# Splitting the last tile's quarter stores into 120 and 8 partitions in a batched 64 x 64 matmul

## The chip, the cores and the metric

The kernel runs on one core of one Trainium2 chip. The metric is the device time of one execution in microseconds (us), taken as the median of several executions. The core has five engines with a queue of instructions each: PE (matrix multiplication), DVE and ACT (elementwise work and copies), POOL and SP. POOL, SP and ACT also issue DMAs; the data of all of them is moved by the same 16 DMA engines.

## The reference

```python
a = np.random.randn(1024, 64, 64).astype(np.float32)
b = np.random.randn(1024, 64, 64).astype(np.float32)

def reference(a, b):
    return np.matmul(a, b).astype(np.float32)
```

1024 independent products of 64 x 64 matrices: 33.55 MB are read and 16.78 MB written.

## The kernel before, in words

The batch is cut into 16 tiles of 64 products (t = 0 to 15; n_t is 16). For a tile, b is loaded as 128 partitions (`load_b`, line 93, alternately on SP and ACT), and cast to bf16 (`cast`, line 140). Two tiles share one load of a (`load_a`, line 69), which is regrouped, transposed on PE against an identity (`transpose`, line 115) and spread by DVE into a block-diagonal form (`spread`, line 128). `multiply` (line 158) runs 64 matmuls of 128 x 64 per tile into PSUM, and `evacuate` (line 171; the copies are line 177) copies the results from PSUM into `o_sb`, a tile of 128 partitions with 8 groups `gh` of 256 fp32 each, so 1 KB per partition and group. In DRAM each of these 1 KB pieces is contiguous, and pieces of neighbouring groups are 128 KB apart.

The order of the work is written out by hand (`tc.manual_schedule()`); each engine's queue holds its instructions in that order. Stores are held back by one tile: `multiply` puts closures into `held[t]`, and `store` (line 154) calls them. Each calls `put(lo, n)` (line 165), which issues the DMA of groups lo to lo + n - 1 on line 166. `store_queue` (line 64) chooses the queue:

- tiles 0 to 13: one whole store of 1 MB each, on POOL;
- tile 14: two halves of 512 KB, both on SP;
- tile 15, the last: four quarters of 256 KB; the first and third (lo = 0 and 4) on ACT, the second and fourth (lo = 2 and 6) on SP.

The last tile's results are copied out of PSUM in the same four quarters, the first and third by ACT, the second and fourth by DVE (four copies of 64 x 256 for each), and a quarter's store waits for its copies.

The framework gives each DMA that is issued on SP or ACT one of eight completion semaphores, in turn. A DMA whose semaphore was used before first waits until that earlier DMA has landed. In the kernel before, tile 14's two stores have semaphores 3 and 4, and the four quarters 5, 6, 7 and 0; their previous users are loads that landed long before.

Of the kernel before, what the change touches and what calls it, by code (L numbers as in the profile page):

```python
# [13 lines left out]
def kernel(  # L14
# [27 lines left out]
    o_v = out.rearrange("(t gh x) (mo w) n -> t (x mo) gh (w n)", gh=8, x=8, w=4)  # L42
# [21 lines left out]
    def store_queue(t, lo):  # L64
        if t < n_t - 2:
            return nc.gpsimd
        return nc.scalar if t == n_t - 1 and lo % 4 == 0 else nc.sync
# [90 lines left out]
    def multiply(t):  # L158
        at_bd = bd_tiles[t % N_BD][:].rearrange("p j g wl h mo -> p j g (wl h mo)")
        at_bd = at_bd.bitcast(bf16).rearrange("p j g (c u) -> p j g c u", u=2)  # L160
        b_bf = bbf_tiles.pop(t)
        last = t == n_t - 1
        o_sb = o_pool.tile([128, 8, 2, 2, 64], fp32, name="o_sb")

        def put(lo, n):
            store_queue(t, lo).dma_start(  # L166
                out=o_v[t, :, lo : lo + n, :],
                in_=o_sb[:, lo : lo + n].rearrange("p gh j wl n -> p (gh j wl n)"),
            )

        def evacuate(o_ps, gh, n, copies):

            for par in range(2):
                for wl in range(2):
                    src = o_ps[64 * wl : 64 * wl + 64, :, par, :, :]
                    dst = o_sb[64 * par : 64 * par + 64, gh : gh + n, :, wl, :]
                    copies[2 * par + wl](dst, src)  # L177

        for half in range(2):
            if not last:  # L180
                o_ps = o_psum.tile([128, 4, 2, 2, 64], fp32, name="o_ps")
            for g8 in range(8):
                if last and g8 % 4 == 0:
                    o_ps = t_psum.tile([128, 2, 2, 2, 64], fp32, name="at_ps")
                g = 8 * half + g8
                gl = (g8 % 4 if last else g8) // 2
                for j in range(2):
                    for u in range(2):
                        nc.tensor.matmul(  # L189
                            o_ps[:, gl, g % 2, j, :],  # L190
                            at_bd[:, j, g, :, u],
                            b_bf[:, g, 64 * u : 64 * u + 64],
                            start=(u == 0),
                            stop=(u == 1),
                        )
                if last and g8 % 4 == 3:
                    copy = nc.scalar.copy if g8 == 3 else nc.vector.tensor_copy
                    evacuate(o_ps, g // 4 * 2, 2, [copy] * 4)
            if not last:
                copies = [nc.scalar.copy] * 4  # L200
                if half and t % 2:
                    copies[2:] = [nc.vector.tensor_copy] * 2
                evacuate(o_ps, 4 * half, 4, copies)
        if last:
            held[t] = [lambda q=q: put(2 * q, 2) for q in range(4)]
        else:
            whole = t < n_t - 2
            held[t] = [lambda q=q: put(q, 8 if whole else 4) for q in ([0] if whole else [0, 4])]
# [78 lines left out]
```

## Time and profile before

| what | value |
|---|---|
| median of 8 executions | 134.88 us (134.53 to 135.39) |
| the profiled execution, its own time | 134.85 us |
| its span, first to last instruction | 133.1 us |
| DVE busy | 94.7 us (71%) |
| ACT busy | 87.9 us (66%) |
| PE busy | 62.9 us (47%) |
| moved by DMA | 45.01 MB, mean 338 GB/s |
| quarter stores on SP: from issue to landing, median | 7.1 us |
| quarter stores on ACT: from issue to landing, median | 5.6 us |

The page of the profile shows one execution. Its second part cuts the span into 40 slices; a digit is the busy share of a slice in tenths. The third part lists the DMA queues (q0 is POOL's, q1 SP's and q10 ACT's; q8 and q14 fetch instructions) with packets, MB and the time that their packets took as a share of 16 engines' span. The fourth follows the chain of work that ended last back from the end. The fifth and sixth list groups of instructions and DMA issues by line. Other views cut the span into stretches that are chosen, or list what one line does in a window. In a fence, "x4" is a count of instructions.

### The profile page before, as it was taken

What the parts mean: (1) busy time and instruction counts of PE and PEld (TensorE: products, weight loads), DVE (VectorE), ACT (ScalarE), POOL (GpSimd) and SP (SyncE); (2) the same over time, 40 slices, a digit from 0 to 9 for tenths busy, and PEclk for the clock granted to TensorE, in tenths of its full rate; (3) what the DMA queues carried; (4) which work ended last, traced back from release to release, by engine and by line L of the source; (5) the groups of instructions that cost most, each with busy time, mean ns of one, the idle gap of its engine ahead of it and who ended that gap; (6) DMA issues with size and microseconds to landing.
All of it is one profiled execution on the core that took longest, in us unless ns stands there. A gap on an engine that the chain in (4) does not pass through costs nothing.

```text
span 133.1 us, 2837 instructions
## 1 busy us (share of the span) xinstructions
PE 62.9 (47%) x1152; PEld 59.8 (45%) x1152; DVE 94.7 (71%) x120; ACT 87.9 (66%) x161; POOL 33.1 (25%) x43
## 2 busy tenths in 40 slices
PE   0006306950089385099418960946098355861000
PEld 0006206940088375098418950935097354850000
DVE  5930499009998719994999799949999995988000
ACT  3125424999036999959495979585969969089800
POOL 8991000420090071252133021302120402210000
PEclk9999965896557999757985698699959955599555
DMA  3999999999999999999999999999999999999991
GB/s 70 373 335 310 306 313 277 284 306 328 324 304 404 320 322 328 399 384 398 316 280 368 408 390 358 305 310 386 393 398 388 394 393 392 401 403 401 381 341 38
DMA packets 19021, 45.01 MB, mean 338 GB/s; under 512 B 1088, under 2 KB 3136, under 8 KB 19008
## 3 DMA queue, kind: packets, MB, share of 16 engines
q0 software_dynamic: 6832, 20.19, 50.2%
q1 hardware_dynamic: 7120, 14.68, 30.5%
q10 hardware_dynamic: 5056, 9.96, 19.8%
q8 instruction: 9, 0.15, 0.4%
q14 instruction: 4, 0.03, 0.1%
HBM read 33.55 MB, written 16.78 MB: 378 GB/s over the span
## 4 chain that ended last, share of the span: by engine, by line
DMA 54%; DVE 14%; ACT 13%; PE 7%; issue 5%; SPq 1%; ACTq 0%; DVEq 0%
DMA b_sb<-in_b_dram 54%; ACT o_sb L177 9%; DVE at_bd L133 6%; PE o_ps L189 4%; DVE o_sb L177 3%; PE at_ps L120 3%; DVE b_bf L144 3%; ACT at_sb L123 2%; ACT b_bf L144 1%; SPq L90 1%; DVE a_bf L108 1%; ACT b_bf L151 1%; DVE a_bf L111 0%; SPq L96 0%; ACTq L166 0%
## 5 line engine op out<-in xcount | busy, mean ns | idle before, releaser
L177 ACT COPY o_sb<-o_ps 64x512 f32<-64x512 f32 x106 | 61.5, 580 | 10.6 <-PE o_ps L189 9.3
L189 PEld LDWEIGHTS <-at_bd 128*128 128x128 bf16 x1024 | 41.8, 112 | 41.0 <-DVE b_bf L144 26.6
L189 PE MATMUL o_ps<-b_bf,at_bd 128*128 128x64 bf16 x960 | 42.0, 215 | 36.8 <-DVE b_bf L144 24.7
L133 DVE COPY at_bd<-at_sb 32x1024 f32<-32x1024 f32 x64 | 47.0, 734 | 14.0 <-ACT at_sb L123 11.9
L166 POOL DMA_DIRECT2D out_dram<-o_sb x14 | 15.7, 1122 | 56.6 <-ACT at_sb L123 23.1
L120 PE MATMUL at_ps<-identity,a_bf 128*128 128x128 f32 x128 | 20.3, 326 | 19.3 <-ACT a_bf L105 11.1
L120 PEld LDWEIGHTS at_ps<-identity,a_bf 128*128 128x128 f32 x128 | 18.5, 174 | 19.3 <-issue 19.3
L144 DVE CAST b_bf<-b_sb 128x2048 bf16<-128x2048 f32 x14 | 17.9, 1276 | 9.9 <-DMA b_sb<-in_b_dram 9.7
L123 ACT COPY at_sb<-at_ps 128x512 f32<-128x512 f32 x32 | 17.5, 589 | 10.2 <-PE at_ps L120 7.5
L73 POOL DMA_DIRECT2D a_sb<-in_a_dram x21 | 13.4, 652 | 26.6 <-DVE a_bf L108 19.0
L177 DVE COPY o_sb<-o_ps 64x512 f32<-64x512 f32 x14 | 9.6, 689 | 0.3
L108 DVE COPY a_bf<-a_sb 128x3072 bf16<-128x3072 bf16 x7 | 6.7, 951 | 0.0
L105 ACT CAST a_bf<-o_sb 128x1024 bf16<-128x1024 f32 x2 | 2.1, 1045 | 5.1 <-DMA o_sb<-in_a_dram 5.1
L111 DVE CAST a_bf<-a_raw 128x1024 bf16<-128x1024 f32 x7 | 4.8, 685 | 0.0
L144 ACT CAST b_bf<-b_sb 128x2048 bf16<-128x2048 f32 x1 | 1.9, 1897 | 4.1 <-DMA b_sb<-in_b_dram 4.1
L217 DVE MEMSET at_bd<- 128x4096 f32 x1 | 3.5, 3472 | 0.8 <-issue 0.8
L105 DVE CAST a_bf<-o_sb 128x1024 bf16<-128x1024 f32 x2 | 2.7, 1355 | 1.8 <-DMA o_sb<-in_a_dram 1.8
L177 DVE COPY o_sb<-at_ps 64x256 f32<-64x256 f32 x8 | 3.4, 421 | 0.5 <-PE at_ps L189 0.4
L151 ACT CAST b_bf<-b_sb 128x512 bf16<-128x512 f32 x2 | 1.1, 615 | 3.5 <-DMA b_sb<-in_b_dram 3.5
L177 ACT COPY o_sb<-at_ps 64x256 f32<-64x256 f32 x8 | 2.9, 366 | 0.1
L214 ACT ACT_TABLE_LOAD x1 | 1.3, 1283 | 2.3 <-issue 2.3
L189 PE MATMUL at_ps<-b_bf,at_bd 128*128 128x64 bf16 x64 | 2.0, 193 | 1.2 <-DVE at_bd L133 1.2
(12 smaller groups left out, 6.1 us busy)
## 6 DMA issues: line engine op xcount, KB each, us to landing
out_dram<-o_sb POOLq DMA_DIRECT2D x14, 1024.0 KB, 21.7
a_sb<-in_a_dram POOLq DMA_DIRECT2D x21, 256.0 KB, 16.2
a_raw<-in_a_dram SPq DMA_DIRECT2D x7, 512.0 KB, 18.7
o_sb<-in_a_dram SPq DMA_DIRECT2D x2, 512.0 KB, 5.9
o_sb<-in_a_dram ACTq DMA_DIRECT2D x2, 512.0 KB, 7.1
out_dram<-o_sb SPq DMA_DIRECT2D x2, 512.0 KB, 6.9
out_dram<-o_sb SPq DMA_DIRECT2D x2, 256.0 KB, 7.1
out_dram<-o_sb ACTq DMA_DIRECT2D x2, 256.0 KB, 5.6
```

Of the source, the lines that this page charges most:

```text
L73: nc.gpsimd.dma_start(out=a_sb[:, h, :, :].rearrange("p v k -> p (v k)"), in_=a_v[s, h])
L105: copy(a_bf[:, :, h, :], a_sb[h].rearrange("p (v k) -> p v k", v=16))
L108: nc.vector.tensor_copy(a_bf[:, :, 0:3, :], cast_sb[:].rearrange("p h v k -> p v h k"))
L111: nc.vector.tensor_copy(a_bf[:, :, 3, :], raw[:])
L120: nc.tensor.transpose(at_ps[:, vo, :], a_cols[:, 4 * vo + 2 * j + wl, :], identity[:])
L123: nc.scalar.copy(at_tiles[s][:, j, :, wl, :, :], at_ps[:].rearrange("p vo (g mp) -> p g mp vo", mp=4),)
L133: nc.vector.tensor_copy(bd[rows, :, :, :, h, :].rearrange("p j g wl mo -> p j (g wl) mo"), at_tiles[t // 2][rows, :, half, :, :, :].rearrange(
L144: (nc.vector.tensor_copy if t else nc.scalar.copy)(b_bf[:], b_sb[:])
L166: store_queue(t, lo).dma_start(out=o_v[t, :, lo : lo + n, :], in_=o_sb[:, lo : lo + n].rearrange("p gh j wl n -> p (gh j wl n)"),)
L177: copies[2 * par + wl](dst, src)
L189: nc.tensor.matmul(o_ps[:, gl, g % 2, j, :], at_bd[:, j, g, :, u], b_bf[:, g, 64 * u : 64 * u + 64], start=(u == 0), stop=(u == 1),)
L217: nc.vector.memset(bd_tiles[0][:], 0.0)
```

## The change

`put` takes its 128 partitions in one store as before, unless the tile is the last one. For the last tile it issues two stores one behind the other on the same queue: partitions 0 to 119, and partitions 120 to 127.

```diff
         def put(lo, n):
-            store_queue(t, lo).dma_start(
-                out=o_v[t, :, lo : lo + n, :],
-                in_=o_sb[:, lo : lo + n].rearrange("p gh j wl n -> p (gh j wl n)"),
-            )
+
+            cuts = [0, 120, 128] if last else [0, 128]
+            for p0, p1 in zip(cuts[:-1], cuts[1:]):
+                store_queue(t, lo).dma_start(
+                    out=o_v[t, p0:p1, lo : lo + n, :],
+                    in_=o_sb[p0:p1, lo : lo + n].rearrange(
+                        "p gh j wl n -> p (gh j wl n)"
+                    ),
+                )
```

The stores are line 169 of the changed kernel. Its last tile has eight stores instead of four: on ACT the first quarter's large and small piece, then the third's; on SP the second's and then the fourth's. With the two halves of tile 14 ahead of them, ten stores take the eight semaphores in turn: 3 and 4 (tile 14), then 5 and 7 (second quarter, large and small), 6 and 0 (first quarter), 1 and 3 (fourth), 2 and 4 (third). The listing of the built program shows these waits:

```
SP   120x2x256 second quarter, large  [waits DMAHW5, DVE]
SP   8x2x256   second quarter, small  [waits DMAHW7]
SP   120x2x256 fourth quarter, large  [waits DMAHW1, DVE]
SP   8x2x256   fourth quarter, small  [waits DMAHW3]
ACT  120x2x256 first quarter, large   [waits DMAHW6, Activation]
ACT  8x2x256   first quarter, small   [waits DMAHW0]
ACT  120x2x256 third quarter, large   [waits Activation]
ACT  8x2x256   third quarter, small   [waits DMAHW4]
```

## The prediction

> **What bounds the kernel now.** I read the page from the top down: the 40 slices, the queue table, the chain, the issues; then the stretches of the tail, the DMA view of the last microseconds, and the stores one by one.
>
> ```profile
> DMA  3999999999999999999999999999999999999991
> ...
> q8 instruction: 9, 0.15, 0.4%
> ...
> DMA 54%; DVE 14%; ACT 13%; PE 7%; issue 5%; SPq 1%; ACTq 0%; DVEq 0%
> ```
>
> The DMA engines are nine tenths busy or more from the second slice to the last but one: the kernel is a stream of 45.01 MB, and compute only decides what is in the stream. 54% of the chain is a DMA. The chain stops at 125.85 us with an ACT copy; behind it only stores are left. The q8 line matters below: nine instruction fetches take 0.4% of 16 x 133.1 us, so about 0.95 us each (8.5 / 9), and a packet is on one engine.
>
> The tail by stretches (us from the span's start; busy time of PE, PEld, DVE, ACT, POOL; clock, DMA share, GB/s):
>
> ```profile
> 124.00:126.00 2.00, 0.00 (x0) 0.00 (x0) 0.00 (x0) 1.79 (x5) 0.00 (x0) 0.50 1.06 384
> 126.00:128.00 2.00, 0.00 (x0) 0.00 (x0) 0.00 (x0) 0.00 (x0) 0.00 (x0) 0.50 1.08 379
> 128.00:129.00 1.00, 0.00 (x0) 0.00 (x0) 0.00 (x0) 0.00 (x0) 0.00 (x0) 0.50 1.01 350
> 129.00:130.00 1.00, 0.00 (x0) 0.00 (x0) 0.00 (x0) 0.00 (x0) 0.00 (x0) 0.50 0.65 229
> 130.00:131.00 1.00, 0.00 (x0) 0.00 (x0) 0.00 (x0) 0.00 (x0) 0.00 (x0) 0.50 0.20 69
> 131.00:132.00 1.00, 0.00 (x0) 0.00 (x0) 0.00 (x0) 0.00 (x0) 0.00 (x0) 0.50 0.02 8
> ```
>
> From 126 us on no engine computes. All 16 DMA engines are full until 128.6 or so, then they run dry one after the other over 2.7 us. The DMA view of 128.0 to 131.4, in slices of 85 ns, shows how it ends:
>
> ```profile
> GB/s 374 386 362 374 373 386 386 338 325 301 301 277 265 253 253 277 265 229 217 217 193 193 181 181 169 133 84 72 72 60 36 24 24 24 24 24 24 24 24 0
> ```
>
> The last eight slices, from 130.63 to 131.31, hold 24 GB/s, a sixteenth of the 380 before: one engine alone, about 0.7 us behind all others. 24 GB/s is 1,024 B in 43 ns. Why one engine is late the same view for 112 to 134 us suggests: one of the nine q8 packets falls in it (0.3% of 16 x 22 us, 1.06 us). The profile names no engine.
>
> When the stores land I take from the instructions of line 166, cut to a window that holds one each: first the second half of tile 14 (SP), then the last quarter (SP), then the third quarter (ACT).
>
> ```profile
> L166 SPq DMA_DIRECT2D out_dram<-o_sb x1: 378/378/378, 122.8 to 122.8; - x1
> ...
> DMA to landing us min/median/max: 6.6/6.6/6.6
> ```
> ```profile
> L166 SPq DMA_DIRECT2D out_dram<-o_sb x1: 1244/1244/1244, 124.7 to 124.7; - x1
> ...
> DMA to landing us min/median/max: 7.1/7.1/7.1
> ```
> ```profile
> L166 ACTq DMA_DIRECT2D out_dram<-o_sb x1: 379/379/379, 125.9 to 125.9; - x1
> ...
> DMA to landing us min/median/max: 5.7/5.7/5.7
> ```
>
> So tile 14's second half lands at about 129.45, the third quarter at 131.6, the last quarter at 131.75; the remaining 1.35 us to 133.1 are the closing waits and barrier. The execution's own time is 134.85, 1.75 more than its span and 0.03 under the median of 134.88.
>
> **What the Trainium skill says.** (1) DMA: Bandwidth & Descriptors, section on why a DMA increments its semaphore by 16: a DMA runs on the largest number of engines, at most 16, that divides the slowest dimension of both sides, on the lowest-numbered ones. 128 gives 16, 120 gives 15, 8 gives 8. The trace of before has only 128 and cannot confirm it. So engine 15 gets nothing of the last tile, 0 to 7 get one partition more, 8 to 14 the same as now. (2) Same page, Latency and other measured facts: engines 7 and 15 are usually slower in traces. Here one engine is late, but which is not told. (3) SBUF, Door 1: partitions share 16 DMA ports, four by four, of some 27 GB/s each. With 128 partitions each engine has its own port by the page; how 120 are dealt to 15 is not said, and no run here shows it.
>
> **The change, part by part.** *Removed*: four stores of 128 x 2 pieces of 1 KB, 16 on each engine per quarter, 64 in all. *Added*: four stores of 120 x 2 (16 pieces on each of engines 0 to 14) and four of 8 x 2 (two on each of 0 to 7). Compute is unchanged in kind and order; the listings of both programs differ only by the four extra stores. Bytes are the same, 1 MB.
>
> *Engine 15*: 64 x 43 ns = 2.7 us less. It is worth something only if it is the late one. *Engines 0 to 7*: 4 x 2 x 43 ns = 0.34 us more. *Engines 8 to 14*: nothing.
>
> *Issues.* One store costs its queue 0.38 to 1.26 us (SP's four: 0.39, 0.38, 1.26, 1.24; ACT's: 0.40, 0.38). On SP the small piece of the second quarter stands ahead of the last quarter, which goes out 0.4 to 1.3 us later, at 125.0 to 125.9. That is hidden: SP's ring holds data on every engine until 128.6, and with 2 us to its first byte (below) it arrives by 128. If that cover went, the quickest engines would idle for some tenths, and they are 2.7 us ahead of the end. On ACT the small piece of the first quarter goes out behind the large one at about 124.8; the copies of the third quarter (124.73 to 125.85) are already handed to the engine, so that the third quarter's store still goes at 125.9. If they were not, 0.4 us later, still within the 2.7.
>
> *The added waits.* Eight semaphores are used in turn, and a store waits until its semaphore's previous DMA has landed. With ten stores at the end instead of six, the last two go round: the listing of the changed program has the small piece of the last quarter (SP) wait for tile 14's first half (landed 120.45 + 7.2 = 127.65), that of the third quarter (ACT) for tile 14's second half, 129.45. Behind each only the closing waits are queued; but these are what the end waits for. Time to the first byte after an issue: the first load of the kernel, 1.4 us (issued at 0.74, first bytes in the slice of 2.1); ACT's first quarter, 1.9 (issued at 124.36; its queue has no packet to 126.27 and one by 126.32); SP's tile 14, 2.65 (issued at 120.45, first packet by 123.12). I take 1.9, the same queue in the same tail, and keep 1.4 and 2.65. From last byte to landing: 131.31 to 131.7, about 0.35. So ACT's small piece lands at 129.45 + 0.1 (two added packets ahead of tile 14's on eight engines) + 0.05 + 1.9 + 0.09 (two packets) + 0.35 = 131.95, between 131.45 and 132.7, against 131.75 now. SP's could land 1.8 earlier, so its packets just follow its ring's backlog.
>
> *Regrouping.* If eight neighbouring partitions go to one engine, engines can meet at a port. From below nothing (no gain can come of it, the ports being one to an engine now); from above, half of the 2.7 us at some 13 instead of 24 GB/s, +1.0 us. I take 0.1, since the last engine runs alone and neighbours fall out of step.
>
> *Sum.* The late engine is among the lower eight: 131.75 + 0.34 = 132.1. ACT's small piece, due at 131.95, queues behind that engine's own last packets and adds no more. With 0.1 for regrouping the end moves 0.44: 134.85 + 0.44 = 135.3.
>
> **The rivals.** *A, faster: the spared engine is the late one.* The others end at 130.63; with 0.34 on the lower eight and 0.35 to landing, 131.3. Tile 14's second half then lands up to 0.7 earlier on the spared engine (16 packets of ACT's no longer between), and ACT's small piece lands at about 131.3 to 131.5. 134.85 - 0.45 = 134.4 (134.1 to 134.65). It decides if the late engine is number 15. For it: (2). Against: the lateness looks like an instruction fetch, about which nothing ties it to 15.
> *B, nearly nothing*: the late engine is one of 8 to 14, or the split does not fall on 15 engines. Only ACT's wait counts, 131.95: 135.05.
> *C, much slower*: ACT's small piece needs SP's 2.65 us, landing at 132.7, or the ports cost the upper bound: +0.95, 135.8. For it: 2.65 is a store of this kernel. Against: by 129.5 the rings are nearly empty.
>
> **How the numbers follow.** Forecast 0.40 (own range 135.0 to 135.6), A 0.30, B 0.12, C 0.18. About 0.3%, 0.40 us, can be told from no change: faster means under 134.48, slower over 135.28. Forecast: 0.25 slower, 0.15 same. A: 0.20 faster, 0.10 same. B: same. C: slower. Together 0.20, 0.37, 0.43. The range runs from 134.3, inside A, to 135.9, the end of C; some 0.15 is left outside.
>
> **What would show it.** Right: the last 24 GB/s stretch is longer or later by 0.3, and the last small store on ACT is issued at about 129.5 and lands near 132. Wrong by A: the lone engine's stretch is gone, and the last landing is before 131.5. By B: the stretch unchanged. By C: DMA share down between 126 and 130, or two empty microseconds ahead of the last 16 KB.

## The result and the profile after

The changed kernel takes 135.9 us (median of 11 runs, 135.52 to 136.53) against 134.95 (32 runs) of the kernel before: a ratio of 1.0073, 95% interval 1.0056 to 1.0091. It is slower by 0.95 us. The forecast was slower by about 0.4; rival C gave this size, 0.95, but not by what came about; the part on the prediction takes this up. The profiled execution took 135.52 us, the quickest of all, with a span of 133.7; in the trace the difference is therefore 0.67 and not 0.95.

The page after, slices and chain:

```profile
DMA  3999999999999999999999999999999999999982
...
DMA 54%; DVE 15%; ACT 13%; PE 6%; issue 5%; SPq 1%; ACTq 0%; DVEq 0%
```

Up to the last copy nothing has moved: ACT's last copy ends at 125.86, before at 125.85. The tail in stretches (columns as in the forecast: us; PE, PEld, DVE, ACT, POOL; clock, DMA share, GB/s):

```profile
124.00:126.00 2.00, 0.00 (x0) 0.00 (x0) 0.00 (x0) 1.80 (x5) 0.00 (x0) 0.94 1.05 377
126.00:128.00 2.00, 0.00 (x0) 0.00 (x0) 0.00 (x0) 0.00 (x0) 0.00 (x0) 0.50 0.97 293
128.00:129.00 1.00, 0.00 (x0) 0.00 (x0) 0.00 (x0) 0.00 (x0) 0.00 (x0) 0.50 0.69 202
129.00:130.00 1.00, 0.00 (x0) 0.00 (x0) 0.00 (x0) 0.00 (x0) 0.00 (x0) 0.50 0.94 269
130.00:131.00 1.00, 0.00 (x0) 0.00 (x0) 0.00 (x0) 0.00 (x0) 0.00 (x0) 0.50 0.89 294
131.00:132.00 1.00, 0.00 (x0) 0.00 (x0) 0.00 (x0) 0.00 (x0) 0.00 (x0) 0.50 0.23 77
```

Two things are new. From 126 to 128 us the engines are still busy (0.97), but they move 293 GB/s where it was 379: the same pieces of 1 KB take longer (by the trace's packet records 54 ns in the mean, 46 before). And from 128 to 129 they are idle for three tenths, where they were full. The DMA view of 128.0 to 131.4 has no lone engine at its end any more; in that stretch the engines are still at work together:

```profile
GB/s 205 205 205 193 181 205 169 181 169 217 265 229 241 241 205 205 229 289 289 265 313 325 325 337 313 277 265 337 337 362 301 289 277 253 229 169 133 145 145 73
```

The stores of line 169, one to a window, show why there is a gap. SP's small piece of the second quarter and then the large piece of the last quarter:

```profile
L169 SPq DMA_DIRECT2D out_dram<-o_sb x1: 1681/1681/1681, 124.7 to 124.7; - x1
```
```profile
L169 SPq DMA_DIRECT2D out_dram<-o_sb x1: 1790/1790/1790, 126.5 to 126.5; - x1
...
DMA to landing us min/median/max: 5.4/5.4/5.4
```

ACT's small piece of the first quarter, the large piece of the third, and the small piece of the third:

```profile
L169 ACTq DMA_DIRECT2D out_dram<-o_sb x1: 1990/1990/1990, 125.0 to 125.0; - x1
```
```profile
L169 ACTq DMA_DIRECT2D out_dram<-o_sb x1: 1320/1320/1320, 127.1 to 127.1; - x1
...
DMA to landing us min/median/max: 5.2/5.2/5.2
```
```profile
L169 ACTq DMA_DIRECT2D out_dram<-o_sb x1: 283/283/283, 129.6 to 129.6; - x1
```

The first small piece on each queue, 16 KB, holds it for 1.7 and 2.0 us; the two last large pieces are issued at 126.5 and 127.1 instead of 124.7 and 125.9. The last small piece goes out at 129.6, right after tile 14's second half has landed (129.57 by the trace's completion records, which note each engine's arrival for each store). Its first arrival is at 131.44 and its last at 132.64, the last of all; before, the last arrival was at 131.72. The same records count 15 arrivals for a piece of 120 partitions and 8 for a piece of 8, beside those that are noted at the issue.

### The profile page after: what moved, and what is told of

It is laid out like the page before. It is cut to its first block, busy times and chain, and to the rows that moved or that the text cites. A ratio compares the mean times of both kernels' runs of the same rounds, so it can differ in the third digit from the quotient of the medians.

```text
span 133.7 us, 2841 instructions
## 1 busy us (share of the span) xinstructions
PE 66.7 (50%) x1152; PEld 63.7 (48%) x1152; DVE 94.6 (71%) x120; ACT 88.0 (66%) x161; POOL 33.2 (25%) x43
## 4 chain that ended last, share of the span: by engine, by line
DMA 54%; DVE 15%; ACT 13%; PE 6%; issue 5%; SPq 1%; ACTq 0%; DVEq 0%
DMA b_sb<-in_b_dram 54%; ACT o_sb L182 9%; DVE at_bd L133 7%; PE o_ps L194 4%; DVE b_bf L144 4%; DVE o_sb L182 3%; PE at_ps L120 2%; ACT at_sb L123 2%; ACT b_bf L144 1%; SPq L90 1%; DVE a_bf L108 1%; ACT b_bf L151 1%; ACTq L169 0%; DVE a_bf L111 0%; SPq L96 0%
## 5 line engine op out<-in xcount | busy, mean ns | idle before, releaser
L194 PEld LDWEIGHTS <-at_bd 128*128 128x128 bf16 x1024 | 43.5, 114 | 39.1 <-DVE b_bf L144 26.3
L120 PE MATMUL at_ps<-identity,a_bf 128*128 128x128 f32 x128 | 22.5, 351 | 18.9 <-ACT a_bf L105 11.1
L120 PEld LDWEIGHTS at_ps<-identity,a_bf 128*128 128x128 f32 x128 | 20.8, 190 | 19.0 <-issue 19.0
L123 ACT COPY at_sb<-at_ps 128x512 f32<-128x512 f32 x32 | 17.5, 590 | 10.5 <-PE at_ps L120 7.6
L194 PE MATMUL at_ps<-b_bf,at_bd 128*128 128x64 bf16 x64 | 3.6, 241 | 1.0 <-DVE at_bd L133 1.0
```

The lines of the kernel that those rows point to most:

```text
L120: nc.tensor.transpose(at_ps[:, vo, :], a_cols[:, 4 * vo + 2 * j + wl, :], identity[:])
L123: nc.scalar.copy(at_tiles[s][:, j, :, wl, :, :], at_ps[:].rearrange("p vo (g mp) -> p g mp vo", mp=4),)
L194: nc.tensor.matmul(o_ps[:, gl, g % 2, j, :], at_bd[:, j, g, :, u], b_bf[:, g, 64 * u : 64 * u + 64], start=(u == 0), stop=(u == 1),)
```

## The experiments

Three theories stood after the profile. **Theory 1, blocked queue**: the small stores hold the large ones back and the engines run short. **Theory 2, grouping**: 120 partitions on 15 engines move slower. **Theory 3, the wait**: the last small stores wait for tile 14 and end last. Each run below was timed beside the kernel before, whose median was 134.94 to 135.03; ratios are to it, with 95% intervals.

### The large pieces first

```diff
-            held[t] = [lambda q=q: put(2 * q, 2) for q in range(4)]
+            held[t] = [
+                lambda q=q, part=part: put(2 * q, 2, part)
+                for part in (slice(0, 1), slice(1, 2))
+                for q in range(4)
+            ]
```

(`put` issues only the piece that `part` names.)

> All eight stores of the changed kernel, but on each queue the two large pieces go ahead of the two small ones. Theory 1 (blocked queue: in the changed kernel a small store holds its queue for 1.7 to 2.0 us, so that the large store behind it goes out 1.2 to 1.8 us late and the engines run short of data at 128 to 129 us): the large stores go out as before the change, at 124.7 and 125.9, the share at 128 to 129 is near 1 again, and most of the 0.95 us comes back, 135.0 to 135.3. Theory 2 (grouping: 120 partitions on 15 engines move slower): stays at 135.9. Theory 3 (the wait for tile 14's landing puts the last small store at the end): the wait is still there, stays at 135.8 to 135.9.

Measured: 137.27 us, ratio 1.0178 (1.0160 to 1.0196). All three theories miss it: the order that should have mended the loss more than doubles it. Its stretches:

```profile
126.00:127.00 1.00, 0.00 (x0) 0.00 (x0) 0.00 (x0) 0.00 (x0) 0.00 (x0) 0.50 0.98 302
127.00:128.00 1.00, 0.00 (x0) 0.00 (x0) 0.00 (x0) 0.00 (x0) 0.00 (x0) 0.50 0.93 248
128.00:129.00 1.00, 0.00 (x0) 0.00 (x0) 0.00 (x0) 0.00 (x0) 0.00 (x0) 0.50 0.97 276
129.00:130.00 1.00, 0.00 (x0) 0.00 (x0) 0.00 (x0) 0.00 (x0) 0.00 (x0) 0.50 0.92 281
130.00:131.00 1.00, 0.00 (x0) 0.00 (x0) 0.00 (x0) 0.00 (x0) 0.00 (x0) 0.50 0.48 125
131.00:132.00 1.00, 0.00 (x0) 0.00 (x0) 0.00 (x0) 0.00 (x0) 0.00 (x0) 0.50 0.26 79
132.00:133.00 1.00, 0.00 (x0) 0.00 (x0) 0.00 (x0) 0.00 (x0) 0.00 (x0) 0.50 0.18 53
```

The gap at 128 to 129 is closed, as theory 1 said, and it does not help. The engines are busy at 250 to 300 GB/s, and then a few of them go on alone, the last until 133.9. Theory 1 as the cause of the loss falls.

### Half of the split, two ways

```diff
-            cuts = [0, 120, 128] if last else [0, 128]
+            cuts = [0, 120, 128] if last and lo >= 4 else [0, 128]
```

> Only the third and fourth quarter are split; the small pieces are the last of their queues, and with eight stores at the end none waits for a store of tile 14. Theory 1: nothing stands behind the small pieces, 134.95 to 135.2. Theory 2: half of the loss, about 135.4. Theory 3: the wait is gone, 134.95.

Measured: 136.06 us, ratio 1.0077 (1.0056 to 1.0098). Nothing is held and nothing waits, and yet the whole loss is there, twice what theory 2 gave for it. The other half:

```diff
+            cuts = [0, 120, 128] if last and lo < 4 else [0, 128]
```

> Only the first and second quarter are split; each small piece stands ahead of a whole quarter of 128 partitions, and none waits for a store of tile 14. Theory 1: the quarters behind go out 1.2 to 1.8 us late as in the changed kernel, 135.5 to 135.9. Theory 2: half of the loss, about 135.4. Theory 3: 134.95.

Measured: 135.48 us, ratio 1.0037 (1.0023 to 1.0051): half the loss, as theory 2 said; theory 1's range began at 135.5, so that this run alone does not tell the two apart.

### The large pieces alone

```diff
+            cuts = [0, 120] if last else [0, 128]
```

> The last tile's quarters store only partitions 0 to 119; the last 8 partitions of that tile are left out, so 64 KB are not stored. Theory 1: no small store, nothing blocked, 134.8 to 134.95. Theory 2: the loss stays, 135.6 to 135.9. Theory 3: no wait, 134.8 to 134.95. If the engine that ends last in the kernel before is the one that is spared by 120 partitions, the last landing comes 0.4 to 0.7 earlier: 134.3 to 134.5.

Measured: 136.49 us, ratio 1.0122 (1.0093 to 1.0151). Four stores as before, no small one, no added wait, 64 KB less to move, and 1.51 us slower (136.49 - 134.98). Of the three only theory 2 expected a loss, and this one is above its range.

```profile
126.00:128.00 2.00, 0.00 (x0) 0.00 (x0) 0.00 (x0) 0.00 (x0) 0.00 (x0) 0.50 0.96 284
128.00:129.00 1.00, 0.00 (x0) 0.00 (x0) 0.00 (x0) 0.00 (x0) 0.00 (x0) 0.50 0.95 262
129.00:130.00 1.00, 0.00 (x0) 0.00 (x0) 0.00 (x0) 0.00 (x0) 0.00 (x0) 0.50 0.80 216
130.00:131.00 1.00, 0.00 (x0) 0.00 (x0) 0.00 (x0) 0.00 (x0) 0.00 (x0) 0.50 0.39 123
131.00:132.00 1.00, 0.00 (x0) 0.00 (x0) 0.00 (x0) 0.00 (x0) 0.00 (x0) 0.50 0.25 87
132.00:133.00 1.00, 0.00 (x0) 0.00 (x0) 0.00 (x0) 0.00 (x0) 0.00 (x0) 0.50 0.16 56
```

Busy engines move less (284 GB/s at 0.96), and they end far apart: a share of 0.25 from 131 to 132 is four engines of sixteen. The completion records say the same: of the last quarter's 15 arrivals (and one at the issue) eleven are in by 130.78, the other four at 131.73, 132.43, 133.00 and 133.27; the third quarter's last is at 133.60. Before, 15 of the last quarter's 16 were in by 130.26, the last at 131.72. While the four go on alone, after 132 us, each of their 1 KB packets takes 46 ns, as before the change: they fell behind earlier.

### What in the grouping costs

Eight stores of all 128 partitions, by group instead of by partition:

```diff
-            held[t] = [lambda q=q: put(2 * q, 2) for q in range(4)]
+            held[t] = [lambda q=q: put(q, 1) for q in range(8)]
```

(with the queue of each quarter kept).

> The last tile's quarters are each split by group instead of by partition: eight stores of 128 partitions x 1 KB, two where the changed kernel has a large and a small one, on the same queues in the same order. Theory 2 in the form that the runs so far leave (ports: 120 partitions are dealt to 15 engines in neighbouring eights, so that engines meet at the same SBUF ports): all 16 engines keep their own ports, and only the time that the added stores hold their queues is left, 135.0 to 135.4. Theory 1 (the number of stores on a queue is what costs): as the changed kernel, 135.8 to 136.0.

Measured: 134.76 us, ratio 0.9990 (0.9980 to 1.0000). Twice the number of stores costs nothing, though the later ones are issued late here too and the last waits for tile 14's second half (issued at 129.27). Then a cut at 64:

```diff
+            cuts = [0, 64, 128] if last else [0, 128]
```

> As the changed kernel, but cut at partition 64: two pieces of 64 partitions, each on all 16 engines (four partitions for each). Ports theory: each piece reaches only half of the ports, two engines at one port all the time, slower than the changed kernel: 136.5 to 138, with a busy share near 1 at about 200 to 250 GB/s. Rival (what costs is that only 15 engines carry the large piece and only 8 the small one): both pieces use 16 engines evenly, 135.0 to 135.4.

Measured: 134.91 us, ratio 0.9993 (0.9980 to 1.0006). The ports theory missed the time. But its last store, when it is alone, does what it said (same columns):

```profile
131.10:131.30 0.20, 0.00 (x0) 0.00 (x0) 0.00 (x0) 0.00 (x0) 0.00 (x0) 0.50 1.03 220
```

All engines are busy, and 220 GB/s come of it. The last store of the split by group holds as many bytes, from all 128 partitions, and moves 357 GB/s at the same share:

```profile
130.20:130.40 0.20, 0.00 (x0) 0.00 (x0) 0.00 (x0) 0.00 (x0) 0.00 (x0) 0.50 1.04 357
```

The Trainium skill, SBUF - State Buffer, Door 1, gives 218 GB/s as what the 8 ports of partitions 0 to 63 can carry; the last piece here is partitions 64 to 127, again 8 ports by that page. So engines do meet at ports, by that count two at each. Here it costs no time, most likely because the engines share the slowing evenly: the records of the last store have all 16 arrivals between 131.76 and 132.00, where before one engine came 1.5 us after the others.

```diff
+            cuts = [0, 112, 128] if last else [0, 128]
```

> As the changed kernel, but cut at partition 112: 112 and 16 partitions, both divisible by 16, so that each piece is on all 16 engines (seven partitions and one). Ports theory: seven neighbouring partitions for an engine share ports as eight do, 135.7 to 136.5. Rival (15 engines instead of 16): 135.0 to 135.3.

Measured: 135.58 us, ratio 1.0043 (1.0028 to 1.0058), a little under the range of the ports theory and above the rival's.

```diff
+                queue = nc.gpsimd if p0 else store_queue(t, lo)
```

> As the changed kernel, but the four small pieces go out on POOL's queue, which is idle by then. SP and ACT have only the large pieces, nothing is held, and no store waits for a store of tile 14. Theory 1 and theory 3: 134.9 to 135.2. Ports theory: nothing keeps the large pieces of the two queues apart, so as the kernel with the large pieces alone, 136.3 to 136.8.

Measured: 136.99 us, ratio 1.0164 (1.0138 to 1.0190). That is above the range: without the holding it is worse still. (The small pieces are late themselves on POOL, 7.1 us from issue to landing, but the last of them is in at 133.40 and the third quarter's large piece at 133.89.)

### Places in DRAM, or engines, or neighbours

The next two write the last tile's 1 KB pieces to other places of its own 1 MB, partitions 4 KB apart instead of 1 KB: once 128 partitions, once 120.

```diff
+    o_moved = out.rearrange("(t y) m n -> t (y m n)", y=64)[n_t - 1].rearrange(
+        "(g p q r) -> p g q r", p=128, g=2, q=4
+    )
...
-                    out=o_v[t, p0:p1, lo : lo + n, :],
+                    out=o_moved[p0:p1, :, lo // 2, :] if last else o_v[t, p0:p1, lo : lo + n, :],
```

> The kernel before, but the last tile's 1 KB pieces go to other places of the tile's own 1 MB in DRAM (neighbouring partitions 4 KB apart instead of 1 KB, the two groups of a quarter 512 KB apart), so the last tile's results are permuted. It is the control of the next run. If the places in DRAM don't matter: 134.9 to 135.1. If pieces that are written at the same time hinder each other by their places in DRAM: another time, slower or faster, which can't be foretold.

> As the control with moved places in DRAM, but only partitions 0 to 119 of the last tile's quarters are stored, on 15 engines; the last 8 partitions are left out and the rest of the tile is permuted. SBUF side (engines meet at the ports that their neighbouring partitions share): the places in DRAM make no difference, the loss against the control is the 1.0 to 1.8 us of the run with the large pieces alone, 136.0 to 136.8. DRAM side (15 engines that start 8 KB apart): with 32 KB between them the loss is another, most likely under 0.5 us: 134.9 to 135.5.

Measured: the control 134.99 us, ratio 1.0002 (0.9989 to 1.0015); with 120 partitions 136.26, ratio 1.0075 (1.0048 to 1.0102). The loss against the control is 1.3 us by the medians and 1.0 by the ratios, at other places too. So these places in DRAM are not the cause, which speaks for the SBUF side.

```diff
+            cuts = [0, 60, 120] if last else [0, 128]
```

> The last tile's quarters are stored as partitions 0 to 59 and 60 to 119, each piece on 15 engines with four neighbouring partitions for each; the last 8 partitions are left out. The number of stores, the holding of the queues and the waits are as in the cut at 64. Neighbouring eights as the cause: with four to an engine it goes as the cut at 64, 134.7 to 135.2. Fifteen engines as such as the cause: as the run with the large pieces alone, 135.8 to 136.5.

Measured: 134.77 us, ratio 0.9986 (0.9975 to 0.9998). Fifteen engines cost nothing when each has four partitions of a piece. The DMA view of this kernel, 128.0 to 132.4 in slices of 110 ns, says two things more:

```profile
GB/s 289 326 372 326 345 298 317 270 214 270 326 307 261 214 168 214 186 196 177 102 102 19 28 28 168 242 279 205 140 130 37 28 19 19 0 0 0 0 0 0
```

At 130.3 to 130.6 one engine works alone (19, 28, 28), as in the kernel before. By the completion records 14 of 15 engines are done with a piece of the second quarter by 128.88 and the last at 130.38: in this execution the late engine is one of the fifteen, not the spared one, and sparing one engine all of the last tile gains 0.14%, at most 0.25%. And behind it comes a second wave, from 130.64 on: the last store, which had waited for tile 14's second half (landed at 129.77). Here the wait is in full view.

### How the loss of the changed kernel is made up

```diff
+            cuts = ([0, 120, 128] if lo < 4 else [0, 120]) if last else [0, 128]
```

> The changed kernel without the small pieces of the third and fourth quarter, whose 8 partitions are left out: eight stores at the end, none waits for a store of tile 14, and the small pieces of the first and second quarter still hold the queues. If the wait of the last small stores is part of the loss: 135.4 to 135.6. If it is hidden: 135.8 to 136.0. If it is worth nothing that the later large stores are held back: as the large pieces alone, 136.3 to 136.6.

Measured: 135.54 us, ratio 1.0046 (1.0031 to 1.0062). Without the last two small stores and their waits the loss is 0.58 instead of 0.95; with the first two, which hold the queues, it is 0.93 less than that of the large pieces alone (1.51), though 32 KB more are stored. By the intervals the 0.37 between the changed kernel and this one is good to some 0.3.

The run takes the last small pieces away together with their wait. Which of the two costs the time, the completion records show. In the changed kernel the last arrivals of the third quarter's large piece and of the two last small ones are 132.24, 132.43 and 132.64. With only the third and fourth quarter split, where nothing waits for tile 14, they are 132.73, 132.93 and 133.12: the same 0.4 us. So the price is that of two small pieces behind a large one on the engine that ends last, some 0.2 us each, and the wait is hidden: in the packet records of the changed kernel the last 1 KB packets, up to 132.06, follow one another without a gap, as one engine's do (no record names the engine). The cut at 64 and the split by group, whose last stores wait in the same way (issued at 129.59 and 129.27), lose nothing.

```diff
+            cuts = [0, 112] if last else [0, 128]
```

> The last tile's quarters store only partitions 0 to 111, on 16 engines with seven neighbouring partitions for each; the last 16 partitions are left out. No small store, no added wait. Ports theory: sevens start at another place of the ports on each engine and meet less than eights, 135.0 to 135.6. If any piece whose partitions are dealt in neighbours of more than four costs the same: 136.2 to 136.6.

Measured: 135.48 us, ratio 1.0037 (1.0019 to 1.0054), with runs from 134.69 to 136.45: sevens lose about a third of what eights do. Here the small pieces bring no gain by holding the queues: with them, in the cut at 112, it was 135.58.

```diff
-        return nc.scalar if t == n_t - 1 and lo % 4 == 0 else nc.sync
+        return nc.sync
```

(with the large pieces alone)

> The large pieces alone, all four on SP's queue; the last 8 partitions are left out. If the loss needs large pieces of two queues in flight together: 134.9 to 135.4. If the pieces of one queue, on engines that are at different places of it, are enough: 136.0 to 136.6.

Measured: 135.52 us, ratio 1.0040 (1.0026 to 1.0053). It lies between the two answers: one queue is enough for 0.56 of the 1.51 us. As one queue also issues later, it doesn't tell whether two queues' pieces must meet or the stores must merely be close.

The last run looked for a quicker kernel: only the third and fourth quarter by group, so that no store waits.

> A candidate that may beat both kernels: only the third and fourth quarter are split by group (128 partitions x 1 KB), on the same queues, so that eight stores stand at the end and none waits for a store of tile 14. If what the split by group gains is that the last data of the engines is spread more finely: as there or better, 134.5 to 134.8. If the gain there is chance: 134.9 to 135.1.

Measured: 134.97 us, ratio 0.9999 (0.9985 to 1.0013). No gain; the split by group of all quarters, with 0.1%, is the best seen that stores the whole result, and its interval reaches no change.

## Why the prediction was wrong in size

The direction and the place were right: slower, in the tail, compute untouched. The size was 0.44 against 0.95.

**Regrouping: the step that failed.** It stood as "I take 0.1, since the last engine runs alone and neighbours fall out of step", with 1.0 as the upper bound (its own figures give 1.1). In the changed kernel, without the last two small pieces, the loss is 0.58; with the large pieces alone it is 1.51, above that bound. The reason given was false: the engines do not fall out of step evenly. With the large pieces alone four engines end 1 to 2.5 us behind the other eleven, and the late engines are the end. The packet records show how. Of the 1 KB packets from 126 to 130 us none took 90 ns or more in the kernel before, in the control with moved places and in the split by group; it was 1.1% with 60 and 60 partitions, 3.4% with the cut at 64, 8.0% with 112 alone, 8.4% in the changed kernel and 10.5% with 120 alone, where single packets took up to 286 ns; 46 is the usual.

Shown is that pieces of 120 and of 112 partitions cost and pieces of 60, 64 and 128 do not; that neither the number of engines nor the places in DRAM that were tried make the difference; and that a lone store of 64 partitions moves 220 GB/s with all engines busy. That an engine gets neighbouring partitions, eights of 120 and fours of 60, fits all runs, but no record names the partitions of an engine. All kernels with fours have eight stores, so that their later stores go out late as in the changed kernel; four stores in fours were not run. Why some engines fall so far behind, and which, is open.

**The issues.** "0.4 to 1.3 us later ... That is hidden" was wrong in both parts: the last quarter went out 1.8 us later, and the cover is gone (0.69 at 128 to 129). On ACT the third quarter's store did not still go at 125.9 but at 127.1. Yet the holding goes with a gain of 0.93, presumably since the later large pieces then meet fewer of the earlier ones; the three kernels of 120 partitions without it took 136.49, 136.99 and 137.27. With 112 partitions there was no such gain, so this is not settled. Nor is why an issue takes that long; with the large pieces first, a small store took longer still:

```profile
L169 SPq DMA_DIRECT2D out_dram<-o_sb x1: 3935/3935/3935, 125.7 to 125.7; - x1
```

**The wait.** It was found where the forecast had it: issue at 129.6 (forecast 129.5). The last landing was 132.64 and not 131.95, but the first arrivals came at 131.44; the others stood behind large pieces on their engines. That the wait vanishes behind the last engine's own packets, as the sum had it, was right.

**The late engine.** The sum put 0.34 on it, for four small pieces of two packets each. In the changed kernel two of the four came behind the last large piece and cost 0.37 (0.40 by the arrivals), as each took some 0.2 us with its completion where 0.09 had been counted. That the term came out is luck. The engine that ends last there carries small pieces; whether it is the late one of the kernel before is not known. The reading of the lateness as an instruction fetch fits. The fetch packet runs from 121.93 to 122.95 in the kernel before; the last arrival of tile 11's store (120.40) comes 0.09 us after the one before it, those of tiles 12, 13 and 14 (124.02 to 129.47) 0.7 to 1.2 us. That the engine which a dealing to 15 leaves out is not the late one is shown for one execution, and leaving it out gained 0.14% (at most 0.25%) where A wanted 0.3%; rival A is out. The chance of 0.30 for A was too high.

**Rival C.** Its 0.95 is the measured size by chance: SP's 2.65 us to the first byte were not seen on ACT's last piece (1.85 to its first arrival), and the large pieces alone cost 1.51, more than C's bound for the ports.

**The engines.** 15 for 120 and 8 for 8, as the Trainium skill, DMA: Bandwidth & Descriptors, has it in the section on the semaphore's 16: the arrivals agree.

So the forecast's 0.34 + 0.10 stands against 0.37 for the last two small pieces and 0.58 for all the rest, which is 1.51 with the large pieces alone less the 0.93. The parts add up to 0.95 because they were taken as differences; that is no test of them.

## What to carry to other kernels

Before a store is cut by partition, ask which partitions each DMA engine will get: here a cut that seems to give each engine eight neighbours cost more than the store count, the wait or the spared engine, while a cut along the free dimension cost nothing. A small piece behind a large one is not free either: it added 0.2 us at the end where its packets alone take 0.09. When a resource that the profile does not show is bounded from two sides, take the middle and not the kind end, unless a row of the profile speaks for that end. And a lone engine at the end of a stream is no sign which engine it is; spare one without changing anything else before you build on it.

## What the runs showed of the hardware that was not expected

- A store of 64 partitions, alone, moved 220 GB/s with all 16 engines busy, against 357 for as many bytes from 128 partitions; spread among other stores it cost no time at all (ratio 0.9993).
- Four stores of 120 partitions were 1.51 us slower than four of 128, with 6% fewer bytes in them.
- The size of a store does not set how long its issue keeps the queue: it was 0.28 to 3.9 us for 16 KB, the long ones right behind larger stores, and 0.38 to 0.39 for 512 KB in the kernel before. What sets it is open.
- A single 1 KB packet took up to 286 ns with pieces of 120 partitions, against 46 as a rule; in the kernel before none took over 79 (both from 126 to 130 us).
